# All direct tiles of a block's tokens ahead of its products, and casts behind the copies that empty banks: one change to an encoder step's input projection

## The chip, the cores and the metric

The kernel runs on one core of a Trainium2 chip. The metric is the device time of one execution in microseconds; of several runs the median is given. A core has TensorE (PE in the profile, its weight loads PEld), VectorE (DVE), ScalarE (ACT), GpSimd (POOL) and SyncE (SP), which issues the transfers. Each engine works through its own list of instructions in order.

## The reference, cut to what matters

One layer of a streaming encoder on 2048 prompt tokens and 8 x 16 sample tokens, with a model width of 1024:

```python
def trunk_layer(x, ...):
    qm, km, vm, om, ip, fp, qa, ka, va = split_in(x @ w_in)
    ...                                   # mLSTM on qm, km, vm, gates ip, fp; windowed attention on qa, ka, va
    mix = jnp.concatenate([hm, ha], axis=-1) @ w_out
    h = layer_norm(DEEPNORM_ALPHA * x + mix, ln1_g, ln1_b)
    f, conv_rows = conv_ffn(h, conv_prev, w_up, w_conv, b_conv, w_down)
    y = layer_norm(DEEPNORM_ALPHA * h + f, ln2_g, ln2_b)
```

The change touches the first product, `x @ w_in`. Its columns are 4 x 512 for the mLSTM, 512 attention queries, and 264 others: the 8 gates, 128 attention keys and 128 values.

## The kernel before

**Precision.** All inputs are float32. A matmul takes operands in a rounded form, so every operand is split into a high half (a cast on ScalarE, `nc.scalar.copy`) and a low half (a subtraction on VectorE), and each product is three matmuls: high x high, high x low, low x high. Weights are split by `split` (lines 218 and 219), tokens by `x_steps` (566 and 567), the sample tokens by `x_single` (578, 579).

**Blocks.** The input projection (`i_dense`) goes over four blocks of 512 prompt tokens. A block's tokens lie in four quarters, loaded by `x_load` (line 538): quarter 1 is features 0 to 511 of the first 256 tokens, quarter 2 the same features of the other 256 tokens, quarter 3 features 512 to 1023 of the first 256 tokens, quarter 4 the rest. With the first block come the 128 sample tokens (tile number 4 of this block).

**Products.** The five groups of 512 columns are multiplied in a seven-product scheme for 2 x 2 quarters: products 1 to 7 use sums and differences of token quarters (made on VectorE, lines 548 to 558) and of weight quarters (`split_first`, 504 to 523), and need seven products in place of eight. A product is 24 matmuls (`i_product`, line 705). Three banks, A, B and C, collect them, and `i_after` takes the results out: line 780 copies A into B behind product 1, others copy a bank into a buffer (764, 772, 761) or a bank into a bank (800). In the first block, products 1, 2, 5 and 4 are followed by 12 matmuls for the sample tokens (line 715).

**Direct tiles.** The 264 other columns are multiplied directly, 24 matmuls for a tile of 128 tokens (`i_direct`, line 731): eight slices of the features, three matmuls each. Tiles 0 and 1 read the split quarters 1 (first four slices) and 3, tiles 2 and 3 the split quarters 2 (called `b12`) and 4. `i_keys` copies the bank out (739, 740), rotates the keys (`rope`, 869 to 872) and stores them. A direct tile uses bank A when its number is even, C when odd; tile 4 of the first block has a bank of its own.

**Order.** TensorE's order is written out in `i_begin` as a list of items: `("t", block, tile, weights)` and `("p", block, group, product)`. For the first block it is: tiles 2 and 3, product 1 of group 0, tile 4, the other products, and tiles 0 and 1 at the end; then tiles 2 and 3 of the second block. Side chains (the mLSTM and the attention) are woven in between by a planner's costs. On the other engines a scheduler orders instructions; `issue_after(ins)` orders what is issued inside it behind `ins` on the engine of `ins`. `advance` issues transfers and splits of weights as far ahead as buffers allow: a ring of eight half buffers, so four products ahead at most.

**Buffers.** A split token quarter has a named buffer of its own, one deep (`x_slot`); `b12` uses the buffer of product 4's tokens, so block two's `b12` can be written only once product 4 of the last group of block one has read its tokens.

**The start.** `i_dense` loads quarter 2, the four parts of the direct weights, quarter 4, the sample tokens, and then quarter 1, the first weights of group 0, and quarter 3. Nine matmuls on zeros (`warm_up`, line 328) go ahead of everything.

Of the kernel before, what the change touches and what calls it, by code (L numbers as in the profile page):

```python
# [205 lines left out]
class Prog:  # L206
# [131 lines left out]
    def i_begin(self):  # L338
# [196 lines left out]
    def x_load(self, b, *qs):  # L535
        for q in qs:
            self.xr[b, q] = r = self.x_raw(q)
            self.nc.sync.dma_start(r, self.a["xq"][b][(q - 1) // 2, (q - 1) % 2])

    def x_steps(self, b, *steps):  # L540
# [3 lines left out]
        for s in steps:  # L544
# [14 lines left out]
            else:  # L559
# [3 lines left out]
                n = 4 if (b, s) == (0, "b12") else 1  # L563
# [24 lines left out]
    def i_dense(self):  # L588
# [5 lines left out]
        self.x_load(0, 2)  # L594
        for _ in range(3):
            self.next_raw()
        self.x_load(0, 4)
# [3 lines left out]
        self.rope_load(IBLOCKS[0][2], 2)  # L601
# [12 lines left out]
        self.x_steps(0, 2, "t3", 7, "t2", 6)  # L614
# [8 lines left out]
        for item in self.items:  # L623
# [9 lines left out]
            if item[0] == "t":  # L633
# [3 lines left out]
                if b not in self.gates:  # L637
                    self.gates[b] = self.tp.tile([P, 5, 8], F32, name="gates", tag="gates", bufs=2)
                ps = self.bank([P, 512], "pg") if ti == 4 else self.ib[ti % 2 * 2]
                yield from self.i_direct(b, ti, e, ps)  # L640
                self.i_keys(b, ti, ps)
                if ti == 1:
# [4 lines left out]
                    after = [6, b + 1]  # L647
                elif ti == 3 and b or ti == 4:
# [18 lines left out]
            if (g, s) == (1, 6):  # L667
# [12 lines left out]
            with self.tc.issue_after(behind) if behind and b == 0 else nullcontext():  # L680
# [38 lines left out]
    def i_direct(self, b, ti, e, ps):  # L719

        mm = self.nc.tensor.matmul
        for k in range(KD):
# [33 lines left out]
    def i_out(self, b, g, i, j, src):  # L756

        nc = self.nc
        ev = src if i else self.zev()
        if g == 3:  # L760
            nc.scalar.activation(ev, src, AF.Tanh, scale=0.5)
            nc.vector.tensor_scalar_add(ev, ev, 1.0)
        elif not i:
            nc.scalar.copy(ev, src)
        if g == 2:
            self.rope(ev, IBLOCKS[b][2 * j], 2)
        self.i_store(b, g, i, j, ev)

    def i_after(self, b, g, s):
        nc, V = self.nc, self.nc.vector  # L770
        A, B, C = self.ib
        copy = lambda d, x: nc.scalar.activation(d, x, AF.Copy, scale=KSCALE) if g < 2 else nc.scalar.copy(d, x)
# [1414 lines left out]
```

## Time and profile before

| what | value |
|---|---|
| median of 3 runs | 2311.37 us (2309.41 to 2311.43) |
| the profiled execution | 2306.19 us |
| its span | 2304.4 us |
| TensorE busy | 2279.1 us (99%) |
| VectorE busy | 1807.5 us (78%) |
| ScalarE busy | 1272.6 us (55%) |
| DMA, mean | 274 GB/s |

A row of the timeline gives the start, the duration, the engine, the line, the operation, and the written and read tiles; `x3` means three in a row under one duration from the first start to the last end. Neighbours overlap at their ends, so the pace is the distance of starts. In brackets stands the idle time of the engine ahead of it and what ended that. `w` is a split weight, `wraw` a raw one, `xr` a raw token quarter, `oh` and `ol` its high and low half, `dps` the banks, `zev` a buffer for results, `rb` one of the rotation.

### The profile page before, as it was taken

The numbers are of one execution on the slowest core, as the hardware profiler recorded it, in microseconds if no ns is written. First come the engines' busy times: TensorE is split into PE (matmuls) and PEld (weight loads), VectorE is DVE, ScalarE is ACT, GpSimd is POOL, SyncE is SP. The second block draws the span as 40 slices with busy tenths as digits, with TensorE's granted clock in tenths as the row PEclk, the third lists the DMA queues.
The fourth block names the chain that finished last, engine by engine and source line by source line (L and its number), as shares of the span: only waits on it lengthen the run. The fifth ranks groups of instructions, "written<-read, shape, count | busy, mean of one in ns | idle before, by whom it ended". The sixth has DMA issues, their size and how long they took to land.

```text
span 2304.4 us, 39746 instructions
## 1 busy us (share of the span) xinstructions
PE 2279.1 (99%) x14293; PEld 2093.5 (91%) x14293; DVE 1807.5 (78%) x3075; ACT 1272.6 (55%) x2377; POOL 272.7 (12%) x509
## 2 busy tenths in 40 slices
PE   8999999999999999999999999999999999999998
PEld 8999999999877778999999999999999988888876
DVE  8787587787688878998778777678766786895987
ACT  4453476776766656555656555555555544444442
POOL 0001001000011210211112100003111200100100
PEclk9999999999999999999999999999999999999999
DMA  7988999999987757888778889978998786756742
GB/s 265 320 303 298 311 321 342 312 305 345 313 285 241 239 196 278 306 320 307 277 276 279 302 307 308 320 263 290 318 293 262 230 294 214 256 167 222 254 154 84
DMA packets 300165, 632.38 MB, mean 274 GB/s; under 512 B 47868, under 2 KB 141120, under 8 KB 299968
## 3 DMA queue, kind: packets, MB, share of 16 engines
q1 hardware_dynamic: 295296, 616.14, 77.8%
q0 software_dynamic: 3520, 10.56, 1.4%
q10 hardware_dynamic: 1152, 3.15, 0.4%
q8 instruction: 113, 1.85, 0.3%
q14 instruction: 84, 0.69, 0.1%
HBM read 458.11 MB, written 171.64 MB: 273 GB/s over the span
## 4 chain that ended last, share of the span: by engine, by line
PE 81%; DVE 4%; DMA 1%; issue 1%; ACT 1%; POOL 0%; SPq 0%; DVEq 0%; ACTq 0%; POOLq 0%
PE dps L1874 19%; PE fup L1874 19%; PE dps L705 7%; PE fup L2084 7%; PE dps L2084 6%; PE fht L2084 6%; PE dps L223 3%; PE dps L224 2%; PE dps L225 2%; PE ppo L1349 1%; PE psc L1304 1%; PE ppt L1343 1%; PE dps L731 1%; PE fht L1698 1%; DVE w L219 1%
## 5 line engine op out<-in xcount | busy, mean ns | idle before, releaser
L1874 PE MATMUL dps<-hh,uw 128*128 128x384 f32 (+1 forms) x1848 | 478.0, 328 | 2.1 <-DVE u L1905 2.1
L1874 PE MATMUL fup<-hh,uw 128*128 128x384 f32 (+1 forms) x1848 | 478.0, 328 | 0.0
L1874 PEld LDWEIGHTS dps<-hh,uw 128*128 128x128 f32 x1848 | 330.0, 188 | 2.4 <-DVE u L1905 2.4
L1874 PEld LDWEIGHTS fup<-hh,uw 128*128 128x128 f32 x1848 | 330.0, 188 | 0.0
L1931 DVE SCALAR_TENSOR_TENSOR cc<-u,cw,cc 128x768 f32<-128x768 f32 (+1 forms) x264 | 257.9, 977 | 63.7 <-ACT cc L1929 56.9
L1874 PE MATMUL fup<-hl,uw 128*128 128x384 f32 (+1 forms) x924 | 302.7, 328 | 0.9 <-DVE hl L219 0.9
L1874 PE MATMUL dps<-hl,uw 128*128 128x384 f32 (+1 forms) x924 | 302.3, 327 | 0.0
L705 PE MATMUL dps<-w,oh 128*128 128x256 f32 x1344 | 254.2, 284 | 0.0
L218 ACT CAST uw<-wraw 128x1024 fp32r<-128x1024 f32 x126 | 123.2, 978 | 231.4 <-PE dps L2084 122.4
L219 DVE TENSOR_TENSOR w<-wraw,w 128x1024 fp32r<-128x1024 f32 (+2 forms) x167 | 189.3, 1140 | 67.0 <-ACT w L218 64.6
L218 ACT CAST w<-wraw 128x1024 fp32r<-128x1024 f32 (+2 forms) x167 | 163.0, 984 | 121.3 <-PE dps L705 63.4
L705 PEld LDWEIGHTS dps<-w,oh 128*128 128x128 f32 x1344 | 210.4, 188 | 10.9 <-issue 8.1
L219 DVE TENSOR_TENSOR uw<-wraw,uw 128x1024 fp32r<-128x1024 f32 x126 | 142.4, 1130 | 65.7 <-ACT uw L218 64.0
L705 PE MATMUL dps<-w,ol 128*128 128x256 f32 x672 | 187.8, 279 | 0.0
L1874 PEld LDWEIGHTS fup<-hl,uw 128*128 128x128 f32 x924 | 173.5, 188 | 1.6 <-DVE hl L219 1.5
L2084 PE MATMUL fup<-uw,fu 128*128 128x512 f32 x726 | 173.7, 396 | 0.0
L1874 PEld LDWEIGHTS dps<-hl,uw 128*128 128x128 f32 x924 | 173.5, 188 | 0.0
L705 PE MATMUL dps<-oh,w 128*128 128x256 f32 x896 | 169.7, 284 | 3.6 <-DVE w L219 1.3
L2084 PE MATMUL dps<-uw,fu 128*128 128x512 f32 x660 | 165.3, 396 | 1.1 <-DVE uw L219 1.1
L2084 PEld LDWEIGHTS fup<-uw,fu 128*128 128x128 f32 x726 | 136.3, 188 | 33.1
L1929 ACT ACTIVATE cc<-u,cw 128x768 f32<-128x768 f32 (+1 forms) x132 | 132.2, 1001 | 49.2 <-DVE u L1911 23.9
L2084 PEld LDWEIGHTS dps<-uw,fu 128*128 128x128 f32 x660 | 123.8, 188 | 31.5 <-DVE uw L219 1.5
(318 smaller groups left out, 4577.9 us busy)
## 6 DMA issues: line engine op xcount, KB each, us to landing
uw<-zw SPq DMA_DIRECT2D x176, 512.0 KB, 5.0
zw<-uw SPq DMA_DIRECT2D x88, 512.0 KB, 3.5
w<-zws SPq DMA_DIRECT2D x72, 512.0 KB, 5.9
wv<-wup SPq DMA_DIRECT2D x66, 512.0 KB, 4.6
wraw<-wi SPq DMA_DIRECT2D x65, 512.0 KB, 6.1
wraw<-zt SPq DMA_DIRECT2D x60, 512.0 KB, 3.9
wraw<-wdn SPq DMA_DIRECT2D x45, 512.0 KB, 4.5
wraw<-wo SPq DMA_DIRECT2D x40, 512.0 KB, 4.7
```

Of the source, the lines that this page charges most:

```text
L218: nc.scalar.copy(hi, src)
L219: nc.vector.tensor_sub(lo, src, hi.bitcast(F32))
L223: mm(out, ah, bh, start=start, stop=False)
L224: mm(out, ah, bl, start=False, stop=False)
L225: mm(out, al, bh, start=False, stop=stop)
L705: mm(o, l, r, start=s in (1, 7) and c == k == i == 0, stop=k == 3 and i == 2, skip_group_check=True)
L731: mm(o, x, w, start=k == i == 0, stop=k == KD - 1 and i == 2, skip_group_check=True)
L1304: nc.tensor.matmul(ps[kvh][:, j, :nk], q[rs, j0 + j], k[rs, sel], start=i == 0, stop=i == 2)
L1874: mm(ps, l[:, k], r[:, k], start=s in (1, 7) and k == 0 and i == 0, stop=k == 3 and i == 2, skip_group_check=True)
L1929: S.activation(c[:, v], u[:, 2:2 + n], AF.Identity, bias=w[3], scale=w[2])
L1931: V.scalar_tensor_tensor(c[:, v], u[:, i:i + n], w[i], c[:, v], op0=ALU.mult, op1=ALU.add)
L2084: mm(ps, l[:, k, c], r[:, k], start=s in (1, 4, 7) and u == 0 and k == 0 and i == 0, stop=u == nu - 1 and k == n - 1 and i == 2, skip_grou ...
```

## The change

It has two parts. All direct tiles of the first block now stand ahead of its products, and tiles 0 and 1 run by halves of the features: first slices 0 to 3 of tile 0, then of tile 1, then slices 4 to 7 of both. The loads and splits at the start are reordered for it: quarter 1 first, in two transfers between the parts of the direct weights, then quarter 3, 2 and 4. Quarter 1 is split in four pieces, as quarter 2 was; quarter 2 is now split whole. The two tiles are gone from the end of the first block, so tiles 2 and 3 of the second block follow its last product directly. The second part: `i_after` returns the copy that empties the bank for most products, in all blocks, and the splits that `advance` issues behind the product are ordered behind that copy on ScalarE; before, only product 1 of group 0 in the first block had that.

```diff
 if b == 0:
-    it += [("t", 0, i, -1) for i in (2, 3)]
+    it += [("t", 0, i, -1) for i in (1, 2, 3)]
     it += [("p", 0, 0, 1), ("t", 0, 4, -1), ("p", 0, 0, 2), ...]
...
-it += [("t", b, i, b) for i in (0, 1)]
+if b:
+    it += [("t", b, i, b) for i in (0, 1)]
 if b + 1 < nb:
     it += [("t", b + 1, i, b) for i in (2, 3)]
...
 def x_load(self, b, *qs):
     for q in qs:
         self.xr[b, q] = r = self.x_raw(q)
-        self.nc.sync.dma_start(r, self.a["xq"][b][(q - 1) // 2, (q - 1) % 2])
+        x = self.a["xq"][b][(q - 1) // 2, (q - 1) % 2]
+        n = 2 if (b, q) == (0, 1) else 1
+        for i in range(n):
+            k = slice(i * 4 // n, (i + 1) * 4 // n)
+            self.nc.sync.dma_start(r[:, k], x[:, k])
...
-                n = 4 if (b, s) == (0, "b12") else 1
+                n = 4 if (b, s) == (0, 1) else 1
...
 def i_dense(self):
     self.next_raw()
-    self.x_load(0, 2)
-    for _ in range(3):
+    self.x_load(0, 1)
+    self.next_raw()
+    self.x_load(0, 3)
+    for _ in range(2):
         self.next_raw()
-    self.x_load(0, 4)
+    self.x_load(0, 2, 4)
...
-    self.x_steps(0, "b12")
-    for _ in range(3):
+    self.x_steps(0, 1)
+    self.next_split()
+    self.x_steps(0, 2)
+    for _ in range(2):
         self.next_split()
-    self.x_steps(0, 3)
+    self.x_steps(0, "b12", 3)
     self.x_single(1, 2)
-    self.x_load(0, 1)
     self.next_raw()
-    self.x_load(0, 3)
-    self.x_steps(0, 1)
     self.advance()
-    self.x_steps(0, 2, "t3", 7, "t2", 6)
+    self.x_steps(0, "t3", 7, "t2", 6)
...
+        if b == 0 and ti == 1:
+            for h in range(2):
+                for i in range(2):
+                    yield from self.i_direct(b, i, e, self.ib[i * 2], (h,))
+            self.i_keys(b, 0, self.ib[0])
+            self.i_keys(b, 1, self.ib[2])
+            self.advance()
+            continue
...
+        elif (b, ti) == (1, 2):
+            self.x_steps(b, 1, 2)
...
-    with self.tc.issue_after(behind) if behind and b == 0 else nullcontext():
+    with self.tc.issue_after(behind) if behind else nullcontext():
         self.advance()
...
-def i_direct(self, b, ti, e, ps):
+def i_direct(self, b, ti, e, ps, halves=(0, 1)):
-    for k in range(KD):
+    for k in [4 * h + i for h in halves for i in range(4)]:
...
 def i_after(self, b, g, s):
     elif s == 6:
         self.u2 = self.zev()
-        copy(self.u2, B)
+        return copy(self.u2, B)
     elif s == 2:
-        self.i_out(b, g, 0, 0, A)
+        return self.i_out(b, g, 0, 0, A)     # returns its copy
     elif s == 5:
         u4 = self.zev()
-        copy(u4, B)
+        emptied = copy(u4, B)
         ...
+        return emptied
     elif s == 3:
-        self.i_out(b, g, 0, 1, B)
+        emptied = self.i_out(b, g, 0, 1, B)
         if g + 1 < NG:
-            nc.scalar.copy(B, A)
+            emptied = nc.scalar.copy(B, A).ins
+        return emptied
```

Further edits go with it: the end of the first block is counted from its last product, and its rotation tables are loaded at the start.

More of the change, by code (lines that the diff above doesn't have):

```diff
@@ L600, in i_dense @@
         self.angles = {}
-        self.rope_load(IBLOCKS[0][2], 2)
+        for i in (0, 2):
+            self.rope_load(IBLOCKS[0][i], 2)
         self.rope_load(NPT, 1)
         self.next_split()
-        self.x_steps(0, "b12")
-        for _ in range(3):
+        self.x_steps(0, 1)
+        self.next_split()
+        self.x_steps(0, 2)
+        for _ in range(2):
             self.next_split()
-        self.x_steps(0, 3)
+        self.x_steps(0, "b12", 3)
         self.x_single(1, 2)
-        self.x_load(0, 1)
         self.next_raw()
-        self.x_load(0, 3)
-        self.x_steps(0, 1)
         self.advance()
-        self.x_steps(0, 2, "t3", 7, "t2", 6)
+        self.x_steps(0, "t3", 7, "t2", 6)
         self.x_single(4)
@@ L666, in i_dense @@
                 self.t_setup()
-            if (g, s) == (1, 6):
+            if (b, g, s) == (0, last, 4):
+                after = [6, 1]
+            if b and (g, s) == (1, 6):
                 self.rope_load(IBLOCKS[b][0], 2)
@@ L759, in i_out @@
         ev = src if i else self.zev()
+        emptied = None
         if g == 3:
-            nc.scalar.activation(ev, src, AF.Tanh, scale=0.5)
+            emptied = nc.scalar.activation(ev, src, AF.Tanh, scale=0.5).ins
             nc.vector.tensor_scalar_add(ev, ev, 1.0)
         elif not i:
-            nc.scalar.copy(ev, src)
+            emptied = nc.scalar.copy(ev, src).ins
         if g == 2:
@@ L771, in i_after @@
         A, B, C = self.ib
-        copy = lambda d, x: nc.scalar.activation(d, x, AF.Copy, scale=KSCALE) if g < 2 else nc.scalar.copy(d, x)
+        copy = lambda d, x: (nc.scalar.activation(d, x, AF.Copy, scale=KSCALE) if g < 2 else nc.scalar.copy(d, x)).ins
         def add(u):
@@ L796, in i_after @@
         elif s == 3:
-            self.i_out(b, g, 0, 1, B)
+            emptied = self.i_out(b, g, 0, 1, B)
             if g + 1 < NG:
-                nc.scalar.copy(B, A)
+                emptied = nc.scalar.copy(B, A).ins
+            return emptied
     def i_batch(self, g):
```

## The prediction

> **What bounds the kernel now.** I read the page first, then the busy time by stretches, then TensorE's timeline of the first 60 us beside those of ScalarE and VectorE, then the same three at the border between the first two blocks of tokens.
>
> ```profile
> span 2304.4 us, 39746 instructions
> PE 2279.1 (99%) x14293; PEld 2093.5 (91%) x14293; DVE 1807.5 (78%) x3075; ACT 1272.6 (55%) x2377; POOL 272.7 (12%) x509
> ```
>
> TensorE is busy 2279.1 of 2304.4 us. The number of matmuls stays as it is, so the change can only win from the 25 us in which TensorE is idle, or from time at a reduced clock, and only where it moves work into such places. The stretches show where they lie (the figure behind the comma is TensorE busy, the third from the end the granted clock).
>
> ```profile
> 0.00:10.00 10.00, 6.69 (x21) 4.70 (x21) 5.88 (x18) 5.59 (x10) 0.31 (x5) 1.00 0.79 278
> 10.00:18.50 8.50, 7.50 (x37) 7.20 (x37) 6.83 (x14) 4.66 (x11) 0.00 (x0) 0.60 1.03 419
> 38.50:46.00 7.50, 5.30 (x28) 4.68 (x27) 7.46 (x9) 4.53 (x6) 0.00 (x0) 0.77 0.84 288
> ```
>
> The mean of 0.60 over 8.5 us is 0.40 / 0.5 x 8.5 = 6.8 us at half clock; 0.77 over 7.5 us is 3.45 us. Each microsecond at half clock is half a microsecond lost. So of the first 46 us, 5.1 us are lost to the clock, and TensorE is idle for 6.5 us in these three stretches. This is the place to look at.
>
> ```profile
> 1.98 4.21 PE L328 MATMUL dps<-zero 128*128 128x512 f32 x9 [1.98 <-DVE zero L323]
> ...
> 8.43 0.39 PE L731 MATMUL dps<-w,oh 128*128 128x264 f32 x1 [0.48 <-DVE w L219]
> ...
> 10.45 0.71 PE L731 MATMUL dps<-w,oh 128*128 128x264 f32 x2 [1.14 <-ACT oh L566]
> 11.71 0.59 PE L731 MATMUL dps<-w,ol 128*128 128x264 f32 x1 [0.55 <-DVE ol L567]
> ...
> 39.45 0.39 PE L705 MATMUL dps<-oh,w 128*128 128x256 f32 x1 [0.68 <-ACT w L218]
> ...
> 40.79 0.50 PE L705 MATMUL dps<-oh,w 128*128 128x256 f32 x2 [0.84 <-DVE w L219]
> ...
> 45.86 0.39 PE L705 MATMUL dps<-oh,w 128*128 128x256 f32 x1 [0.69 <-ACT zev L772]
> ```
>
> The warm-up ends about 6.1 us, so the direct tiles cannot start earlier whatever arrives. Then TensorE waits for halves made by ScalarE (the cast) and VectorE (the subtraction). After idle times of 0.48 and 1.14 us the clock falls; after 0.68 and 0.84 us it falls again. The 40.79 wait is the low half of the weights of product 6. VectorE has hardly an idle moment from 14.7 to 46 us, so it sets when those products may run.
>
> **The head, part by part.** What is moved is tiles 0 and 1: 48 matmuls. Four direct tiles run now without a gap at the border of the blocks.
>
> ```profile
> 153.84 1.59 PE L715 MATMUL psx<-w,xs 128*128 128x256 f32 x12
> 155.26 0.40 PE L731 MATMUL dps<-w,oh 128*128 128x264 f32 x2
> ...
> 166.93 0.28 PE L705 MATMUL dps<-oh,w 128*128 128x256 f32 x1
> ```
>
> 96 matmuls from 155.26 to 166.93 are 0.1216 us each, so 48 are 5.83 us. If the head took them free, that would be the gain. First, arrivals:
>
> ```profile
> 4.72 0.40 ACT L566 CAST oh<-xr 128x256 fp32r<-128x256 f32 x1 [2.70 <-DMA xr<-xq]
> 5.38 0.63 ACT L218 CAST w<-wraw 128x528 fp32r<-128x528 f32 x1 [0.26 <-DMA wraw<-wg]
> ...
> 9.35 1.04 ACT L566 CAST oh<-xr 128x1024 fp32r<-128x1024 f32 x1 [0.57 <-DMA xr<-xq]
> 10.70 1.14 ACT L578 CAST xs<-xsr 128x512 fp32r<-128x512 f32 x2 [0.30 <-DMA xsr<-xs]
> ```
>
> ```profile
> wraw<-wg SPq DMA_DIRECT2D x4, 264.0 KB, 4.9
> xr<-xq SPq DMA_DIRECT2D x4, 512.0 KB, 5.1
> ```
>
> All four casts waited for a transfer. Queued before them in order were 512, 776, 2080 and 2592 KB. In the changed queue the sums are 256 (first half of token quarter 1), 520, 776, 1040 (second pair of gate weights), 1552 (quarter 3), 1816, 2080 (last gate weights), 2592 (quarter 2), 3104 (quarter 4). Between the four points that puts the second gate weights at 6.2 us, quarter 3 at 7.7, the last gate weights at 8.5 and 9.35, quarter 2 at 10.7 and quarter 4 at 12.05 (carried on at 1.35 us per 512 KB). These are estimates. The extra issue for the halves lies under the warm-up and costs nothing; without that cover it would delay the queue by one issue, under half a microsecond.
>
> ```profile
> 7.68 1.94 DVE L219 TENSOR_TENSOR w<-wraw,w 128x528 fp32r<-128x528 f32 x3
> ...
> 14.72 0.23 DVE L869 TENSOR_TENSOR rb<-zev,ropet 128x64 f32<-128x64 f32 x1 [1.14 <-ACT zev L739]
> ...
> 15.73 1.23 DVE L567 TENSOR_TENSOR ol<-xr,oh 128x1024 fp32r<-128x1024 f32 x1
> 16.87 1.42 DVE L219 TENSOR_TENSOR w<-wraw,w 128x256 fp32r<-128x256 f32 x4
> ...
> 20.12 1.22 DVE L219 TENSOR_TENSOR w<-wraw,w 128x1024 fp32r<-128x1024 f32 x1 [0.66 <-ACT w L218]
> ...
> 25.07 1.22 DVE L567 TENSOR_TENSOR ol<-xr,oh 128x1024 fp32r<-128x1024 f32 x1
> ...
> 39.52 3.49 DVE L219 TENSOR_TENSOR w<-wraw,w 128x1024 fp32r<-128x1024 f32 x3
> ```
>
> ```profile
> 14.31 0.37 ACT L739 COPY zev<-dps 128x256 f32<-128x256 f32 x1 [2.48 <-PE dps L731]
> ...
> 38.35 3.89 ACT L218 CAST w<-wraw 128x1024 fp32r<-128x1024 f32 x4 [5.30 <-DVE wraw L511]
> ```
>
> These give the prices: a 1024-wide cast 0.97 us, a 1024-wide subtraction 1.14 (three in 3.49, the last 1.22), a 528-wide cast 0.63 and subtraction 0.65, a rotation of keys 1.0 alone, a copy out of the bank 0.37 (0.5 with the gates). Now the new order, by hand. Quarter 3's cast ends at 8.8, its low half at 9.95; the gate weights' low halves, next on VectorE, at 10.6 and 11.25. TensorE does the first halves of tiles 0 and 1 from 6.1; the second gate weights' low half is there at 7.5, so 17 remaining matmuls end at 9.55, and it waits about 1.0 us for 10.6. Tile 0 ends at 12.0, tile 1 at 13.45, tile 2 at 16.35, tile 3 at 19.2, all at full clock. Quarter 4's cast now stands behind tile 0's copy on ScalarE (a wait that the change adds: from 12.05 to 12.6), its low half ends at 14.75. VectorE then has a rotation (1.0), three sample splits and a subtraction (four at 0.65) and 0.3 of the next rotation, reaches the first weights' four quarters at 18.5, ends them at 20.0 (1.42), finishes the rotation and starts the second weights at 20.5 instead of 20.12.
>
> From there to product 6's weights VectorE takes 39.52 - 20.12 = 19.4 us now. Quarter 3's low half, at 25.07 now, is gone (-1.14), and 0.9 us of rotations come in: 19.2 us. So product 6's weights are ready at 20.5 + 19.2 + 1.22 = 40.9, where they are ready at 40.74 now. VectorE's chain stands still; TensorE has 5.83 us more behind it. From 40.9, product 6's other 23 matmuls take 2.7 us at full clock and the 0.69 us for the bank's copy follows as now: product 5 starts at 44.4. I add 0.9 us for some ten hand-overs between engines that the hand count leaves out. That is 45.3 against 45.86, and the gain of the head is 0.56 + 5.83 = **6.4 us**. On the way product (1,1) waits 2 us for its own low half, which product 6's wait absorbs. The other end: if the clock falls in the head as it does now, tiles 0 to 2 run at 0.22 us per matmul to 17.2 us, tile 2 ends 2.5 to 3 us later, and everything queued behind its copy with it, of which 0.5 is made good: 6.4 - 2.2 = 4.2. My head idles 0.4 and 1.0 us with 2 us of work between, less than the 0.48 and 1.14 that close the gate now, so I take 6.4.
>
> **The border, where cover goes.** Behind the last product of the first block (12 sample matmuls from 153.84) came tiles 0 and 1; now tile (1,2) comes at once. Its first tokens use the buffer that this last product reads, so their cast cannot start before.
>
> ```profile
> 154.04 1.05 ACT L566 CAST oh<-xr 128x1024 fp32r<-128x1024 f32 x1 [0.42 <-PE dps L705]
> ```
>
> ```profile
> 153.65 1.23 DVE L567 TENSOR_TENSOR ol<-xr,oh 128x1024 fp32r<-128x1024 f32 x1 [0.21 <-ACT oh L566]
> 154.79 0.69 DVE L778 TENSOR_TENSOR zev<-dps,zev 128x512 f32<-128x512 f32 x1
> 155.39 1.22 DVE L554 TENSOR_TENSOR xr<-xr,wraw 128x1024 f32<-128x1024 f32 x1
> 156.52 1.22 DVE L567 TENSOR_TENSOR ol<-xr,oh 128x1024 fp32r<-128x1024 f32 x1
> ```
>
> Today the cast starts at 154.04, the low half ends at 157.74, and tile (1,2) starts 11.67 / 2 after 155.26, at 161.1: hidden by 3.4 us. After the change the tile is due at 155.26; two matmuls run on the high half, and the third needs the low half. VectorE's program order ahead of it is the previous quarter's low half, a weight split, the bank's addition and a token subtraction: 152.7 + 1.14 + 1.14 + 0.60 + 1.14 + 1.22 = 157.9. TensorE idles 157.9 - 155.5 = **2.4 us**. The bounds are 2.2 (as in today's order) and 3.5 (one more split ahead).
>
> Whether 2.4 us closes the gate costs half a spell of 3.4 us, 1.7 us. The rows differ: 1.52 us in two pieces closed it near 40, but here 2.85 us in one piece did not:
>
> ```profile
> 250.00:260.00 10.00, 7.15 (x76) 6.26 (x74) 2.56 (x6) 4.30 (x12) 1.19 (x2) 1.00 0.87 290
> ```
>
> I take the fall, since the two spells above are the nearer in kind (a wait on a split between dense products): -1.7, with 0 as the other bound. The Trainium skill, "TensorE: Matmul & The Clock Gate", Part 1 and "HAM oscillation", says that half clock follows at least one idle window of about 3.4 us and asks only for no idle gaps over that. By that rule the border costs 2.4 and no more. This trace disagrees at 40 us and agrees at 250.
>
> **The casts behind the copies.** In the program order 54 of ScalarE's 108 bank copies have a weight cast directly ahead; after the change 24. What one such cast costs today:
>
> ```profile
> 327.01 1.04 ACT L218 CAST w<-wraw 128x1024 fp32r<-128x1024 f32 x1
> 327.95 0.59 ACT L772 ACTIVATE zev<-dps 128x512 f32<-128x512 f32 x1
> ```
>
> ```profile
> 328.60 0.38 PE L705 MATMUL dps<-oh,w 128*128 128x256 f32 x1 [0.95 <-ACT mr L1154]
> ```
>
> The copy at 327.95 stands behind the cast and TensorE waits 0.95 us for it. With the copy first it is ready 0.95 us earlier: **-0.9**. The other copies leave TensorE no wait, since another product lies between. A cast moved behind a copy comes 0.59 us later; the split needs the buffer of the same product to be free anyway, and its own product is three products away (24 matmuls at 0.12 each, 8.6 us), so I cost it at nothing. Waits of the side chains, such as the 2.85 us near 250, shift with VectorE's order; I take zero, bounds -2.9 and +2.
>
> **Sum.** -6.4 (head) -0.9 (copies) +2.4 +1.7 (border) = -3.2 us. The profiled execution took 2306.19 us, so 2303.0 for one like it. The median of the runs shown is 2311.37, 5.2 us higher; I carry the difference over: **2308.2 us**. 0.2% is 4.6 us, about what a measurement of this kernel can tell from no change.
>
> **Rivals.** (a) The gate stays open at the border (the rule above, as the row at 250 has it): -4.9, 2306.5. For it, the 2.85 us; against it, the fall at 41. Chance 0.20. (b) The clock falls in the head as today: -3.2 + 2.2 = -1.0, 2310.4. My idle of 1.4 us is close to the 1.52 that was enough. Chance 0.17. (c) The side chain's 2.85 us near 250 closes too, because VectorE's order there has one rotation step less: -6.1, 2305.3. Chance 0.12. (d) The head gives nothing: VectorE's chain, solid from 14.7 us, slips by all 5.83 us with the two tiles ahead of it. Then -0.9 + 4.1 = +3.2, 2314.6. Against it: only two rotations are added to VectorE there. Chance 0.06. (e) Slower: the casts moved behind copies are late. 30 of them at 0.59 us are 17.7 us if all lose their cover; from 14 on the result is slower than 0.2%; half of them give 8.9 - 3.2 = +5.7, 2317.1. Against it: a lead of 8.6 us less about 2.2 for cast and subtraction. Chance 0.07. My forecast has 0.38.
>
> The range leaves out (d), (e) and the far end of (c): 2303.0 to 2313.5. Faster by over 0.2% (under 2306.8) holds half of (a), nearly all of (c) and a part of the forecast with a smaller border: 0.33. Slower by over 0.2% holds (e): 0.07. Within: 0.60.
>
> **What would show it.** In the changed profile: product 5 of the first block starts near 45.3 us; clock 1.00 over the first 17 us; a wait of TensorE on the low half of tokens of about 2.4 us near 155 us, with a half-clock spell behind it; no 0.95 us wait near 320; no new waits on weight splits in blocks two to four. I am wrong if product 5 starts after 48, if no wait stands at the border, or if waits on weight splits of over 0.5 us recur after 160 us.

## The result, and the profile after

| | before | after |
|---|---|---|
| median of 15 runs | 2309.41 us (2303.73 to 2311.43) | 2313.0 us (2309.64 to 2316.83) |
| the profiled execution | 2306.19 us | 2316.83 us |
| its span | 2304.4 us | 2315.1 us |

The ratio of after to before is 1.0019, 95% interval 1.0013 to 1.0026: slower by 4.4 us (3.0 to 6.0), where 3.2 us less was forecast. (The two medians themselves lie 3.6 us apart; below, times are worked out from ratios.) The forecast of 2308.2 us started from a median of three runs, 2311.37; from that of the 15 runs it would be 2306.2.

The profiled execution of after is the longest of its 15, and that of before is shorter than 14 of its 15, so the two traces differ by 10.7 us, and each step below is checked against ratios too. The trace of before was lucky in one thing: between 46 us and its last 5 us its clock never falls. The other 15 traces of this kernel and its variants have one to five windows of 3.4 us at half clock there, after five.

The page of after shows the same work, 14293 matmuls, and 3.8 us more under PE.

```profile
span 2315.1 us, 39731 instructions
PE 2282.9 (99%) x14293; PEld 2098.2 (91%) x14293; DVE 1807.3 (78%) x3075; ACT 1272.7 (55%) x2377; POOL 284.7 (12%) x509
```

Next the busy time by stretches: length, then busy time of PE, PEld, DVE, ACT and POOL, granted clock, DMA share, GB/s. First two rows of before, for the two stretches that turned out to matter and that were not shown yet:

```profile
155.00:170.00 15.00, 15.00 (x127) 15.00 (x126) 14.88 (x29) 9.44 (x19) 0.00 (x0) 1.00 0.87 274
330.00:372.00 42.00, 41.49 (x348) 38.28 (x347) 29.17 (x74) 29.76 (x77) 4.77 (x9) 1.00 0.98 348
```

Then five of after:

```profile
0.00:10.00 10.00, 6.53 (x23) 4.98 (x24) 4.90 (x17) 5.12 (x9) 0.31 (x5) 0.98 0.75 267
10.00:18.50 8.50, 8.50 (x60) 8.50 (x60) 6.30 (x10) 4.87 (x10) 0.00 (x0) 0.82 1.04 414
38.50:46.00 7.50, 6.26 (x52) 5.87 (x50) 7.50 (x15) 4.31 (x5) 0.00 (x0) 1.00 0.89 309
155.00:170.00 15.00, 12.60 (x93) 12.39 (x93) 11.99 (x18) 8.14 (x13) 0.00 (x0) 0.89 0.87 291
330.00:372.00 42.00, 36.12 (x287) 33.60 (x285) 26.86 (x72) 26.80 (x73) 5.58 (x7) 0.92 0.85 287
```

The head (first three rows) lost most of its time at half clock: 0.82 where 0.60 stood, 1.00 where 0.77 stood. The border (155 to 170) lost what was forecast, 2.4 us idle and a spell at half clock. The stretch from 330 to 372 us, in the third block of tokens, is the surprise: TensorE idles 5.9 us there in place of 0.5, and the clock is 0.92.

To see where the two traces part, I set the start of the same matmul in both side by side and read the difference, after minus before:

| place (time in before) | difference there |
|---|---|
| first matmul behind the moved tiles, 161 us | -5.4 us |
| behind the border's wait and half clock, 170 us | -1.2 us |
| 263 us: a side chain's wait, there in before too, has a half-clock spell behind it | -0.2 us |
| 330 us: the 0.95 us wait is gone, and 0.8 us from smaller ones | -1.9 us |
| 340 us | +4.4 us |
| 372 us | +5.8 us |
| 640 us | +7.9 us |
| last matmul both have, 2284 us | +10.2 us |

TensorE's own rows in the third block:

```profile
331.21 0.95 PE L1366 MATMUL ppt<-ident,sc 128*128 128x128 f32 x5 [0.60 <-ACT sc L1344]
336.10 0.47 PE L1366 MATMUL ppt<-ident,sc 128*128 128x128 f32 x1 [3.94 <-ACT sc L1344]
```

The eight transposes (`ppt`) of the attention's weights wait for ScalarE's divisions (`sc<-sc,asm`, line 1344, in before 1321). ScalarE's and VectorE's rows say why. In before, ScalarE's divisions (the cast at 327.01 and the copy at 327.95, which the prediction shows, stand behind them) and VectorE's reciprocal (`asm`), which the second four need:

```profile
325.25 1.86 ACT L1321 ACTIVATE sc<-sc,asm 128x128 f32<-128x128 f32 x6
...
323.61 0.18 DVE L1319 RECIPROCAL asm<-asm 128x4 f32<-128x4 f32 x1 [1.90 <-ACT sc L1316]
```

In after:

```profile
325.06 0.58 ACT L793 ACTIVATE zev<-dps 128x512 f32<-128x512 f32 x1
...
327.64 1.99 ACT L218 CAST w<-wraw 128x1024 fp32r<-128x1024 f32 x2
330.75 0.99 ACT L1344 ACTIVATE sc<-sc,asm 128x128 f32<-128x128 f32 x3 [1.12 <-DVE asm L1342]
333.99 1.28 ACT L1190 ACTIVATE hn<-hn,ms 128x128 f32<-128x128 f32 x4 [2.25 <-POOL ms L1184]
335.18 0.56 ACT L784 COPY zev<-dps 128x512 f32<-128x512 f32 x1
335.64 0.40 ACT L1344 ACTIVATE sc<-sc,asm 128x128 f32<-128x128 f32 x1
...
330.49 0.17 DVE L1342 RECIPROCAL asm<-asm 128x4 f32<-128x4 f32 x1
```

In before six of the eight divisions ran in one piece ahead of the cast and the copy, the second pair's four among them. In after the copy goes first, which is what the change says (it runs at 325.06, 2.9 us sooner). But the lists behind it are others. On VectorE the reciprocal comes 6.9 us later (330.49 against 323.61), so three of those four divisions come 4.9 us later (325.25 and two steps of 0.3 us, against 330.75, where ScalarE has waited 1.12 us for `asm`). On ScalarE the fourth stands behind the mLSTM's `hn`, which waits 2.25 us for a result of GpSimd, and behind a copy. TensorE stands in front of that one division for 3.94 us, and its clock is at half for two windows, from 334 to 340.8 us.

### The profile page after: what moved, and what is told of

Its sections match the earlier page's. It is cut to its first block, busy times and chain, and to the rows that moved or that the text cites. A ratio compares the mean times of both kernels' runs of the same rounds, so it can differ in the third digit from the quotient of the medians.

```text
span 2315.1 us, 39731 instructions
## 1 busy us (share of the span) xinstructions
PE 2282.9 (99%) x14293; PEld 2098.2 (91%) x14293; DVE 1807.3 (78%) x3075; ACT 1272.7 (55%) x2377; POOL 284.7 (12%) x509
## 4 chain that ended last, share of the span: by engine, by line
PE 80%; DVE 4%; DMA 2%; issue 1%; ACT 1%; SPq 0%; POOL 0%; DVEq 0%; ACTq 0%; POOLq 0%
PE dps L1897 19%; PE fup L1897 18%; PE dps L724 8%; PE fup L2107 7%; PE dps L2107 6%; PE fht L2107 6%; PE dps L223 3%; PE dps L224 2%; PE dps L225 2%; PE ppo L1372 1%; PE ppt L1366 1%; PE psc L1327 1%; PE dps L750 1%; PE fht L1721 1%; DMA w<-zws 1%
```

## The experiments

All ratios are to the kernel before, run on the same chip in the same session; 0.001 is 2.3 us. Thirteen kernels, after among them, share the head and differ behind it, so the head is read from all of them.

**Which part costs.** Four kernels, the first without the second part, the second with nothing else:

```diff
 # e1_head_only: the change, with these lines as before
-with self.tc.issue_after(behind) if behind else nullcontext():
+with self.tc.issue_after(behind) if behind and b == 0 else nullcontext():
 # and i_out, i_after return what they returned before
```

> The changed kernel without its second part: weight casts are queued as before, nothing behind the bank copies. Theory A (the list order of ScalarE that the second part makes in the blocks two to four puts the fourth division of the attention's sums behind hn's wait, and this is the loss): the 3.94 us wait near 336 is absent, the 2.4 us wait near 158 stays, the 0.95 us wait near 328 comes back; in the profile -5.4 (head) + 4.2 (border) = about -1.2 us against the kernel before. Theory B (it is the shift in time by the head and the border that upsets the side chains, and the order does not matter): the 3.94 us wait is there, and the time is that of the whole change, +4 us.

Measured: 0.9996 (0.9987 to 1.0004), 2308.2 us. The stretch from 330 to 372 us is nearly whole again:

```profile
330.00:372.00 42.00, 40.66 (x337) 36.94 (x335) 27.28 (x72) 29.37 (x76) 4.76 (x9) 1.00 0.95 337
```

```diff
 # e2_casts_only: the kernel before, and
-with self.tc.issue_after(behind) if behind and b == 0 else nullcontext():
+with self.tc.issue_after(behind) if behind else nullcontext():
 # and i_out, i_after return the copies, as in the change
```

> The kernel before with the second part alone: casts behind the copies, direct tiles where they were. Theory A: the wait of about 4 us on the attention's division near 330 is there, with half-clock spells behind it, the 0.95 us wait is gone; +4 to +6 us against the kernel before. Theory B: -0.9 us, no wait over 2 us behind 300 us that the kernel before does not have.

Measured: 1.0020 (1.0012 to 1.0029), 2312.7 us. The second part alone is 4.6 us slower, as much as the whole change, and TensorE's rows from its trace, and its stretch, are those of after:

```profile
334.68 0.47 PE L1347 MATMUL ppt<-ident,sc 128*128 128x128 f32 x1 [3.94 <-ACT sc L1325]
330.00:372.00 42.00, 36.73 (x289) 34.53 (x289) 25.35 (x67) 27.21 (x73) 5.58 (x7) 0.92 0.84 281
```

Theory A holds against B: the wait comes without the shift of the head, and goes without the second part.

```diff
 # e3_border: the change, and
-self.hx[b, s] = h, l = self.x_slot(4 if s == "b12" else s)
+self.hx[b, s] = h, l = self.x_slot((5 if b == 1 else 4) if s == "b12" else s)
-passages = [{1: ["load"], 7: ["t3", 7], 6: ["t2", 6], 3: [3, "t4"], 4: ["b12", "t1"]},
+passages = [{1: ["load"], 7: ["t3", 7], 6: ["t2", 6], 5: ["b12"], 3: [3, "t4"], 4: ["t1"]},
```

> The whole change, but the split of the first tokens of tile (1,2) goes to the buffer of slot 5, which is free one product earlier, and is made behind product 5. Both theories: the 2.4 us wait at the border and the half-clock spell behind it go, -4.1 us against the whole change near 160 us. Theory A: the 3.94 us wait near 336 stays, so the total is near the kernel before (0 to +2 us). Theory B: with the border gone the later times shift by 4 us and that wait may change its size by as much, either way.

Measured: 1.0001 (0.9992 to 1.0009), 2309.4 us: 0.0018 or 4.2 us below the whole change. No wait stands between 150 and 170 us, and the wait of 3.94 us stays (at 331.85 us in this trace). The border's price is as forecast.

```diff
 # e4_casts_block1: the change, and only
-with self.tc.issue_after(behind) if behind else nullcontext():
+with self.tc.issue_after(behind) if behind and b == 0 else nullcontext():
```

> The whole change, but casts are held behind the copies in the first block of tokens only, as the kernel before did for its copies there. Theory A: as the head alone, about -1.2 us against the kernel before; 0.95 us wait near 328 is there, 3.94 us wait is not. Theory B: as the whole change, +4 us.

Measured: 0.9995 (0.9985 to 1.0005), 2307.4 us. Held casts in block one are free; the loss of the second part (0.0024, 5.5 us) comes from the blocks behind it.

**Is it the one division?**

```diff
 # e5_division: the change, and for the attention's first tile
-divided(*z[1])
+with self.tc.high_priority() if t == 0 else nullcontext(): divided(*z[1])
```

> The whole change, and beside it one thing: the second pair of divisions of the attention's first tile (reciprocal and four multiplications) gets the higher priority, so that ScalarE's list has the four multiplications in one run ahead of hn's wait and of the two casts. The casts stay behind the copies. Theory A1 (the one division behind hn's wait carries the loss): the waits of 0.60 and 3.94 us near 331 and 336 and the two half-clock spells behind them go; -6.6 us against the whole change in the profile, about -2.5 us against the kernel before. Theory A2 (the second part costs by many casts that come late, and this division is one of several): the wait goes, but others take its place within the same block; at most -3 us against the whole change, so about +1 us against the kernel before.

(The line covers the reciprocal and the four divisions behind it.) Measured: 1.0003 (0.9994 to 1.0012), 2309.4 us: 3.7 us below the whole change and 0.7 us above the kernel before, close to what theory A2 says. The waits near 331 and 336 go, and 20 us later another one has taken their place. Its rows on TensorE, ScalarE and VectorE:

```profile
353.07 0.39 PE L724 MATMUL dps<-w,oh 128*128 128x256 f32 x1 [2.86 <-ACT zev L784]
...
351.46 0.51 ACT L1339 ACTIVATE sc<-sc,amx 128x257 f32<-128x257 f32 x1 [6.10 <-DVE amx L1334]
...
352.46 0.56 ACT L784 COPY zev<-dps 128x512 f32<-128x512 f32 x1
...
350.60 0.69 DVE L874 TENSOR_TENSOR txy<-txy 128x512 f32<-128x512 f32 x1 [4.21 <-DMA txy<-wdn]
```

Read from the bottom: VectorE waits 4.21 us for a transfer (`wdn`, weights that are prepared for a later stage); behind it stands the attention's maximum (`amx`), which ScalarE's exponentials wait for 6.10 us; behind those stands the bank's copy, and TensorE waits 2.86 us for that, with a half-clock spell after it. The same order of lists is in before, where VectorE waits for this transfer only 0.75 us and TensorE not at all:

```profile
350.57 0.69 DVE L851 TENSOR_TENSOR txy<-txy 128x512 f32<-128x512 f32 x1 [0.75 <-DMA txy<-wdn]
```

The transfer is issued later by SyncE's list, which has changed too. In this kernel:

```profile
342.22 0.33 SPq L868 DMA_DIRECT2D txy<-wdn  x1
```

In e8_border_block1 (below), which runs as far ahead of before at this place:

```profile
340.17 0.38 SPq L868 DMA_DIRECT2D txy<-wdn  x1
```

In e8 VectorE waits 0.44 us for it. Of the 3.8 us more in e5, 2.0 are this later issue; for the rest VectorE comes to the transfer 1.7 us sooner. So A1 falls: mending the division brings half, and the next late thing is a transfer that the same part of the change delayed.

```diff
 # e7_border_division: e3_border and e5_division together
```

> The whole change with both mends, the buffer of slot 5 at the border and the higher priority of the four divisions. If the two losses are separate, they add: -4.1 and -6.6 against the whole change, that is head -5.4 and copies -1 to -1.5 against the kernel before: about -6.5 us, 2302. If the side chains answer to the shift of 4 us with a wait of their own: -3 us.

Measured: 0.9991 (0.9982 to 1.0000), 2307.4 us. Not the sum: a wait of 2.15 us on a copy near 351 us, of the kind of e5, and new ones behind.

**Held casts, or the lists behind them?** The version without any held cast behind block one, with the border mended:

```diff
 # e8_border_block1: e3_border and e4_casts_block1 together
```

> The whole change with the buffer of slot 5 at the border, and casts held behind the copies in the first block of tokens alone. No lists of ScalarE change behind the first block against the kernel before. Head -5.4 us, border nothing, the 0.95 us wait near 328 stays: -5.4 us against the kernel before, 2303.5. If this is not faster by at least 3 us, the head's gain is given back somewhere behind the border.

Measured: 0.9980 (0.9971 to 0.9989), 2303.65 us: 4.6 us (2.5 to 6.7) faster than before, and better than both kernels. From it, casts were held in single places of the later blocks:

```diff
 # e9_border_not3, e10_border_only3, e15_border_4: e3_border, and
-with self.tc.issue_after(behind) if behind else nullcontext():
+with self.tc.issue_after(behind) if behind and b != 2 else nullcontext():        # e9
+with self.tc.issue_after(behind) if behind and b in (0, 2) else nullcontext():   # e10
+with self.tc.issue_after(behind) if behind and b in (0, 3) else nullcontext():   # e15
 # e13_one_cast_5, e14_one_cast_6
+... if behind and (b == 0 or (b, g, s) == (2, 0, 5)) else nullcontext():         # e13
+... if behind and (b == 0 or (b, g, s) == (2, 0, 6)) else nullcontext():         # e14
```

> The buffer of slot 5 at the border, and casts held behind the copies in the blocks one, two and four, not in the third. If the loss of the second part is made in the third block alone (330 to 372 us, where the waits of 3.94 and 2.86 us were): as the version that holds in block one alone, -5 us against the kernel before, or up to 1 us better. If every block pays for held casts: -3 us or worse.

> The buffer of slot 5 at the border, and casts held behind the copies in the blocks one and three only. If the loss of the second part is made in the third block: waits of TensorE over 2 us between 330 and 372 us, and +3 to +5 us against the version that holds in block one alone, so about the kernel before. If not: -5 us, no such wait.

> The buffer of slot 5 at the border, casts held in block one, and one cast more: the one queued ahead of the copy of product (2,0,5), the copy that TensorE waits 0.95 us for near 325 us. This is the gain that the prediction counted, alone. The planner answers it with other lists behind it in the third block (ScalarE 33 lines of difference, VectorE 23, SyncE 8, TensorE none). Theory C1 (the casts themselves cost, each by coming late): one cast of 30 costs next to nothing, the 0.95 us wait goes, -0.9 us against the version that holds in block one alone, about 2302.7. Theory C2 (the lists that the planner writes behind a held cast cost): the 0.95 us wait goes and waits on ScalarE of 0.5 us and more come behind it; +1 to +4 us against that version.

> The same with the cast ahead of the copy of product (2,0,6) held, some 9 us earlier, whose list TensorE does not wait for. ScalarE 24 lines of difference, VectorE 34, SyncE 8, and the division of the attention's sums stands behind two copies more. Theory C1: no change against the version that holds in block one alone. Theory C2: a change of over 1 us, of a sign that the lists set: the divisions come apart as in the whole change, so I say +1 to +4 us.

> The buffer of slot 5 at the border, casts held in the blocks one and four. Lists differ behind 453 us only (ScalarE 163 lines, VectorE 135, SyncE 108). Theory C1: held casts in the fourth block cost as those in the others, a third of the loss of 5 us, +1.5 us. Theory C2: what the new lists cost depends on what stands there; in the whole change the fourth block showed a new wait of 1.1 us on ScalarE at 553 us and lost one of 1.1 us at 516 us, so -1 to +1 us.

| held behind block one | ratio (95%) | median |
|---|---|---|
| nothing (e8) | 0.9980 (0.9971 to 0.9989) | 2303.65 us |
| block four (e15) | 0.9984 (0.9975 to 0.9992) | 2304.3 us |
| one cast, (2,0,6) (e14) | 0.9990 (0.9981 to 0.9998) | 2306.56 us |
| one cast, (2,0,5) (e13) | 0.9990 (0.9981 to 0.9999) | 2307.0 us |
| block three (e10) | 0.9990 (0.9981 to 0.9999) | 2306.96 us |
| blocks two and four (e9) | 0.9995 (0.9986 to 1.0003) | 2307.57 us |
| two, three and four (e3) | 1.0001 (0.9992 to 1.0009) | 2309.39 us |

Of my two expectations for e9 the first failed: without a held cast in the third block the gain of e8 does not come back. I take it that the planner writes the later lists after what it thinks went before, so that casts held in the second block change the third block's lists. That for e10 missed too: no wait of over 2 us stands between 330 and 372 us (the longest is 1.33), and the price is 2.3 us where 3 to 5 were expected. By the ratios a single held cast of the 30 costs 2.3 us, as much as that whole block of them, but neighbours in this table are within each other's intervals; only e8 against e3 is clear of them. So for single blocks and casts the times decide nothing, and their traces must. That of e14 leaves it open: from 330 to 372 us it loses 1.5 us against before where e8 loses nothing, and over all that is behind the moved tiles 1.0 us more than e8. The trace of e13 shows the mechanism with one cast. The intended effect is there: at 328.8 us of before the difference goes from -6.6 to -7.6, the 0.95 us wait is gone. Then comes ScalarE's new list,

```profile
327.35 1.28 ACT L1190 ACTIVATE hn<-hn,ms 128x128 f32<-128x128 f32 x4 [2.32 <-POOL ms L1184]
328.54 0.39 ACT L1146 ACTIVATE wi<-wi 128x128 f32<-128x128 f32 x1
328.83 0.57 ACT L784 COPY zev<-dps 128x512 f32<-128x512 f32 x1
329.30 1.04 ACT L218 CAST w<-wraw 128x1024 fp32r<-128x1024 f32 x1
330.24 0.58 ACT L822 COPY dps<-dps 128x512 f32<-128x512 f32 x1
```

where e8 has

```profile
330.29 0.70 ACT L1190 ACTIVATE hn<-hn,ms 128x128 f32<-128x128 f32 x2 [2.90 <-POOL ms L1184]
330.89 0.56 ACT L784 COPY zev<-dps 128x512 f32<-128x512 f32 x1
331.36 0.40 ACT L1190 ACTIVATE hn<-hn,ms 128x128 f32<-128x128 f32 x1
331.66 0.58 ACT L822 COPY dps<-dps 128x512 f32<-128x512 f32 x1
```

In e13 four steps of `hn`, a `wi` and a weight cast stand ahead of the bank copy (L822) that TensorE needs next:

```profile
330.88 0.53 PE L724 MATMUL dps<-oh,w 128*128 128x256 f32 x1 [1.14 <-ACT dps L822]
```

A wait of 1.14 us and a half-clock spell: 2.6 us given back for 0.95 won. C2 holds for this cast in the trace. e15 says that the same thing behind 453 us costs little (0.0004, within the interval).

**The head by halves.**

```diff
 # e11_whole_tiles: e8_border_block1, and
-for h in range(2):
-    for i in range(2):
+for i in range(2):
+    for h in range(2):
         yield from self.i_direct(b, i, e, self.ib[i * 2], (h,))
```

> The buffer of slot 5 at the border, casts held in block one alone, and tiles 0 and 1 of the first block one after the other, not by halves of the features. Tile 0's second half waits for quarter 3's low half (about 9.95 us) without tile 1's first half (12 matmuls, 1.5 us) as cover. If VectorE's chain sets when product 6 can run, as the prediction has it: product 5 starts within 0.5 us of the version by halves, and the time is the same. If TensorE's own list sets it: 1.5 us later, 3.2 with a half-clock spell.

Measured: 1.0007 (0.9999 to 1.0016), 2310.9 us: 0.0027 or 6.2 us slower than by halves, twice what the worse case said. Product 5 starts at 50.17 us. The fair neighbour by halves is e8, which differs in nothing else and whose clock falls once in the head as this one's does; there product 5 starts at 46.43. Rows of VectorE (the split of the last token quarter, product 6's weights) and of TensorE in e11:

```profile
15.59 1.23 DVE L572 TENSOR_TENSOR ol<-xr,oh 128x1024 fp32r<-128x1024 f32 x1 [2.25 <-ACT oh L571]
...
43.82 3.49 DVE L219 TENSOR_TENSOR w<-wraw,w 128x1024 fp32r<-128x1024 f32 x3
...
42.76 0.38 PE L724 MATMUL dps<-oh,w 128*128 128x256 f32 x1 [1.21 <-ACT w L218]
45.09 0.50 PE L724 MATMUL dps<-oh,w 128*128 128x256 f32 x2 [1.83 <-DVE w L219]
```

The same in e8:

```profile
15.94 1.23 DVE L572 TENSOR_TENSOR ol<-xr,oh 128x1024 fp32r<-128x1024 f32 x1 [2.07 <-ACT oh L571]
...
41.61 3.49 DVE L219 TENSOR_TENSOR w<-wraw,w 128x1024 fp32r<-128x1024 f32 x3
...
42.89 0.50 PE L724 MATMUL dps<-oh,w 128*128 128x256 f32 x2 [0.79 <-DVE w L219]
```

Up to the token split nothing is late in e11; it comes 0.35 us sooner. Behind it VectorE's list is another one: two more sums of weight quarters (lines 507 and 510, 1.14 us each) stand ahead of product 6's weights, which come 2.2 us later. TensorE idles 3.0 us for them in place of 0.8, and a second half-clock spell follows: 2.2 us and another 1.5 make the 3.7 us at product 5. So VectorE's chain sets product 6, as the first theory has it, but the order of the matmuls changes what stands in that chain. What the halves are worth with the lists kept as they are, no run shows, and the other 2.5 of the 6.2 us I have not followed.

**The clock.** Two experiments on the half-clock spells. In the first, TensorE's wait at the border is filled:

```diff
 # e6_fill: the change, and in i_direct behind the second matmul of tile (1,2)
+if (b, ti, k, i) == (1, 2, 0, 1):
+    for n in range(20): mm(self.ib[1][:, :264], xh, wh, start=n == 0, stop=n == 19, skip_group_check=True)
```

> The whole change, and 20 matmuls of 128x264 on operands that are there already, written to a bank that nobody reads, are put into TensorE's 2.4 us wait at the border (20 x 0.12 = 2.4 us). TensorE isn't idle there any more, the data comes as late as before. If the half-clock spell of 3.4 us behind the border comes from that idle time: clock 1.00 over 155 to 170 us and -1.7 us at 170 us against the whole change. If the spell has another cause (the kind of work, or a timer that runs anyway): the clock there stays near 0.9 and the time stays as it is or is some tenths worse.

(The bank is B, and the filler changes the sums that block two's first group adds up there; the work is the same in kind and number.) Measured: 1.0010 (0.9997 to 1.0023), 2311.8 us, and clock 1.00 over 155 to 170 us. But e5, which idles there as long as after does, has the same clock in its trace:

```profile
157.20 0.39 PE L750 MATMUL dps<-w,ol 128*128 128x264 f32 x1 [2.40 <-DVE ol L572]
155.00:170.00 15.00, 12.80 (x109) 12.80 (x110) 12.32 (x18) 8.27 (x13) 0.00 (x0) 1.00 0.95 318
```

Behind the same 2.40 us the clock falls in after and in e4, and behind 2.13 us in e1, but not in e5, so a single filled trace shows nothing. In the traces the clock changes only at multiples of 3.413 us from each other, so I measured that by itself:

```diff
 # e12_gate: the change, and at the end of warm_up
+for n in range(84):
+    for i in range(70): self.nc.tensor.matmul(self.ib[0], z[:, :P], z, start=i == 0, stop=i == 69, skip_group_check=True)
+    for i in range(1 + n % 6): self.nc.scalar.copy(z[:, :64 * (1 + n % 7)], self.ib[0][:, :64 * (1 + n % 7)])
```

> The whole change, with 84 bursts of 70 matmuls of 128x512 on zeros put behind the warm-up, each followed by a chain of one to six copies by ScalarE that the next burst waits for, so that TensorE idles for 0.4 to 3.3 us at 84 places of no fixed distance; some 1.4 ms longer, the time says nothing else. Theory G1, from the traces so far: the clock is set once per window of 3.413 us on a grid that runs through from the start, by the window before; over about 1.8 us of idle time in one window gives half clock in the next. Then idle times under 1.8 us are never followed by a fall, those of 2.4 us in two of three cases, (3.41 - 1.8 + 2.4 - 1.8) / 3.41 = 0.65, and every fall has over 1.8 us of idle time in the window before. Theory G2: it is the length of the idle time alone, with a fixed bound. Theory G3: an idle time of a full window, 3.4 us, is needed, and none of these is followed by a fall.

Measured over the bursts: of 447 windows of 3.413 us, 27 were followed by a fall, and these had 1.81 to 3.39 us of idle time in them; the 394 others at full clock had at most 1.82. Of 28 idle times up to 1.0 us none was followed by a fall, nor any of 26 from 1.1 to 1.7; of those of 2.4 us three of four were. Two of these, both of 2.40 us, by windows of the grid. The first lies over two windows, with 1.58 and 0.83 us in them:

```profile
93.85 0.96 PE L330 MATMUL dps<-zero 128*128 128x512 f32 x3 [2.40 <-ACT zero L331]
...
89.61:93.02 3.41, 1.83 (x9) 1.18 (x7) 0.00 (x0) 1.39 (x4) 0.00 (x0) 1.00 0.00 0
93.02:96.43 3.41, 2.58 (x11) 2.17 (x12) 0.00 (x0) 0.74 (x2) 0.00 (x0) 1.00 0.00 0
96.43:99.84 3.41, 3.41 (x16) 2.82 (x16) 0.00 (x0) 0.00 (x0) 0.00 (x0) 1.00 0.00 0
```

The second lies almost whole in one, 2.28 us:

```profile
854.19:857.60 3.41, 1.13 (x6) 0.59 (x4) 0.00 (x0) 2.06 (x5) 0.00 (x0) 1.00 0.00 0
857.60:861.01 3.41, 3.29 (x8) 2.61 (x9) 0.00 (x0) 0.07 (x1) 0.00 (x0) 0.50 0.00 0
```

For these bursts of matmuls on zeros G1 holds. G2 falls by this pair, and G3 by the 25 falls behind idle times of less than a window. The kernel's own work has falls behind less idle time than that; the last section has them.

## Why the prediction was wrong, step by step

**The head: right.** Forecast 6.4 us, or 4.2 with the clock falling. The traces of the thirteen kernels with this head have product 5 at 44.66 to 45.16 us where the clock stays up (eight of them) and at 45.84 to 46.43 where it falls once (five, after among them); I had said 45.3. The gain against the trace of before, at the tiles that are gone, is 6.5 to 7.0 and 5.2 to 5.9 us. By the ratio it is e8's 4.6 us (2.5 to 6.7). In after:

```profile
8.28 0.39 PE L750 MATMUL dps<-w,oh 128*128 128x264 f32 x1 [1.13 <-ACT w L218]
...
9.02 0.39 PE L750 MATMUL dps<-w,oh 128*128 128x264 f32 x1 [0.35 <-DVE w L219]
...
46.23 0.39 PE L724 MATMUL dps<-oh,w 128*128 128x256 f32 x1 [0.69 <-ACT zev L793]
```

The idle 1.4 us that I named as close to enough (1.13 and 0.35 here) were enough in this execution, and rival (b) and the forecast are the same kernel in different executions, so which of the two a trace shows is luck. The reason given, that VectorE's chain stands still, holds within 0.7 us: the matmul of product 6 that waits for that chain starts at 40.79 us in before and at 41.51 in e5, where the clock stays up, with two more tiles ahead of it. It holds for the lists that came out; in e11 another list moves the same point by 2.2 us. The 0.9 us for hand-overs had no row behind them. The terms listed for product 5 add up to 44.3, not 44.4, and the traces at full clock are 0.4 to 0.9 us above that.

**The border: right, to the tenth.** The wait is 2.40 us where 2.4 was worked out, for the low half that was named:

```profile
158.46 0.39 PE L750 MATMUL dps<-w,ol 128*128 128x264 f32 x1 [2.40 <-DVE ol L572]
...
157.19 1.22 DVE L572 TENSOR_TENSOR ol<-xr,oh 128x1024 fp32r<-128x1024 f32 x1
```

With the fall behind it, the trace lost 4.2 us there for 4.1 forecast, and taking it away (e3) brought 4.2. The fall itself is a matter of where the window lies; by the bound of the bursts it comes at 2.4 us in two of three cases, so 1.1 us on average would have been the better term. Rival (a) was half right. The Trainium skill, "TensorE: Matmul & The Clock Gate", Part 1, has the free-running window of 3.4 us, and the traces agree with 3.413; that it takes a window's length of idle time ("HAM oscillation") they don't: the falls here had 1.37 to 3.39 us of it in the window ahead.

**The casts behind the copies: wrong, and it turned the result.** The term was -0.9 us, with the casts at nothing and the side chains at zero within -2.9 and +2. The -0.9 came as forecast in after and e13, where the 0.95 us wait is gone (in e5, e7 and e10, whose casts are held there too, one of 0.68 to 0.92 us stands in its place), but the part as a whole costs 4.6 us alone (e2) and 5.5 in the whole change (e4). The step that failed is "I cost it at nothing": I priced where a cast runs, and not what the planner does with everything behind it. The casts themselves are not late: in after no wait of TensorE on a weight split stands between 160 us and the end of the input projection. But holding a cast changes the lists of ScalarE, VectorE and SyncE for the side chains behind it, and in the third block, where attention and mLSTM both go through ScalarE, the lists that came out have a reciprocal 6.9 us later and a division behind another chain's wait; TensorE waits 3.94 us for that. My own row at 250 us (2.85 us on a side chain) showed the size that such a wait takes. I bounded the loss at 2 us from nothing in the trace. Nor would my own signs have told me: none of the three by which I was to be wrong came true, since they look at the head, the border and weight splits, and not at what the side chains make TensorE wait for.

**Rival (e), the slower one,** had the right part and the right sign, 2317.1 us with half of all casts late. Its mechanism is not what the traces show: no wait on a weight split recurs behind 160 us (the two on weights, 0.24 us at 394 us and 0.69 us at 582 us, are for a transfer); beside these and the old wait near 250 us, TensorE waits up to 560 us for `sc`, `dps` and `pth`, results of ScalarE. Rival (c) did not come, that wait is 2.62 us long in after; nor did (d).

**The sum by ratios:** head -4.6, border +4.2, second part +4.6 to +5.5, together +4.2 to +5.1; measured +4.4. Each term has some 2 us of uncertainty either way.

What stays open: which of the planner's changes behind the held casts make up the 4.6 us. The traces show three places (the divisions in the whole change, the transfer `wdn` in e5, the bank copy in e13), and mending the first uncovers the second. That re-planned lists are the whole of the 4.6 us is argued from these, not shown.

## What to carry to other kernels

Where a planner or scheduler orders several engines' lists, an ordering constraint is not a local edit: compare the lists of all engines before and after, and look in each for a short step that another chain needs and that now stands behind a long wait. Bound such a term by the longest side-chain wait that the trace has, in both directions, not by zero. And take work off an engine's critical stretch together with the buffer that it covered: here the moved tiles had hidden a buffer's hand-over, and one slot of another buffer gave the 4 us back.

## What the runs showed of the hardware

TensorE's clock is set per window of 3.413 us on a grid that runs on through the kernel and lies differently in each execution: every change of the granted clock in the 17 traces of this case lies on one such grid per trace. A window at half clock costs 1.7 us. What brings it on is idle time in the window ahead of it, and much less than a whole window of it.

In the bursts of e12 the bound was sharp: 1.81 us of idle time did it and 1.82 once did not. By that bound an idle time of 2.4 us pays in two of three executions, (3.41 - 1.8 + 2.4 - 1.8) / 3.41; three of four did in e12, and the clock fell in three of the four traces with the wait at the border (2.13 to 2.40 us). Idle times in the same window add up: 1.13 and 0.35 us in the head of after were followed by a fall.

In the kernel's own work the bound is not sharp. In the other 16 traces 42 windows at full clock were followed by a fall, with 1.37 to 2.92 us of idle time. Thirteen of them had at most 1.78 us: ten in the first 46 us, three (1.38 to 1.44 us) in the third block's stretches of small transposes. Of the windows that no fall followed, 27 had 1.37 us or more, the longest 1.90. So up to 1.36 us in one window were always free here, over 1.90 us never, and what decides between the two no run shows. The same kernel's runs spread by some microseconds, partly for this reason: in the head alone the clock falls in five of the thirteen traces.
